# Encoder block with a 32-expert MoE on one Trainium2 core: the branch of an expert's further slots moved ahead of the preceding expert's four down products

## Chip, cores and metric

One core of one Trainium2 chip. The metric is the device time of one execution in microseconds; the kernel before took 2197.92 us, the median of 3 runs (2194.08 to 2198.09).

## The reference, cut to what matters

A streaming-encoder block in float32: 2048 tokens of 1024 numbers. A mixer (mLSTM heads and differential attention) comes first and is not touched by the change. Then a mixture of experts: a token picks one of 4 groups and 2 of its 8 experts, and each of the 32 experts is a SwiGLU with 512 hidden numbers.

```python
g_sel = jnp.argmax(g_logits, axis=-1)
top_vals, top_idx = lax.top_k(e_in, TOP_K)                # 2 of the group's 8
weights = g_w[:, None] * jax.nn.softmax(top_vals, axis=-1)
...
def expert_block(args):
    xb, e = args
    hid = jax.nn.silu(xb @ w_gate[e]) * (xb @ w_up[e])    # 1024 -> 512
    return hid @ w_down[e]                                # 512 -> 1024
...
y = jnp.sum(y_buf[dest].reshape(T, TOP_K, D) * weights[..., None].astype(h.dtype), axis=1)
```

How many tokens an expert gets is known only on the chip. 4096 slots over 32 experts are 128 on average.

## The kernel before

The mixer and the routing fill the first 1388 us. The rest is one unrolled loop over 32 *places* (L1327 on), and an expert stands at each place; a 33rd pass finishes the last one. The order of experts is worked out on the chip, so that those with over 128 slots alternate with others as far as they go.

**The 128 slots that each expert has.** Large products run in split form: a float32 operand is cut into a high part H (ACT, `split_h`, L66) and the rest L (DVE, `split_l`, L70), and H x H, H x L and L x H are added up in PSUM, 3 matmuls for one. `ffn1` (L1231) makes gate and up in 8 steps `d` of 6 matmuls each; `hidden` (L1211 to L1213) makes the hidden numbers `th`, with tanh on ACT and two operations on DVE. The down product of an expert comes one place later: `turn_h` (L1236) turns its th during steps 0 and 1 of the next expert's ffn1, and `down(0)` to `down(3)` (`ffn2`, L1246, 6 matmuls each) stand behind that ffn1. `emit` writes the result one place later still (d = 2: ACT L1251, then a scatter by POOL, L1255, that adds into `out`). During steps 3 and 5 `turn` (L1204) transposes the tokens of the next place, which POOL gathered into `xg0` (L1193); after step 5 POOL gathers those of the place after it.

**Weights.** Raw weights `R` come by SP's DMA queue (L843, `done`), 1 MB a tile, 6 tiles an expert: 4 of gate and up, 2 of down. `ready` splits a half tile 6 halves ahead of its use, into a ring of 4 tiles (8 halves). Each step of ffn1 and each down calls `ready` once, so ACT and DVE get one split a step, in the order of the program.

**Further slots.** An expert with n > 128 enters the branch `more` (L1371). Its further slots go in quarters of Q = 32 rows (M = 64 for the last two), unsplit, against the raw R: `few_turn_x` transposes the tokens (8 small transposes, L1265; ACT copies them to `xH`, L1267), `few_ffn1` is 64 matmuls (L1276) into a `px` tile in PSUM and the `hidden` of it, `few_turn_h` one transpose (L1282) and a copy by ACT to `hH` (L1283), `few_ffn2` 32 matmuls (L1291) into another of the 2 px tiles, `few_emit` four copies by ACT to `yE` (L1307) and a scaling by POOL (L1308), `few_return` the scatter. Inside, `many` (L1376) is n > 160 and `most` (L1384) n > 192. The engines run their own instruction streams: ACT, DVE, POOL and SP take the same branches for themselves. `mark_branch_hint_location` puts a hint (L1458 in the profile) some way ahead of a branch; the branch's If side is the one that falls through, so an expert of up to 128 slots (a *light* place) *takes* the branch to its Else side. In this run 20 places are light, 6 have one quarter, 4 have two and 2 have four.

**Order around the change.** In program order on each engine: ffn1, down(0), down(1), then the branch. Inside it: small transposes, down(2), few_ffn1 of the first quarter, the inner branch; with two quarters or more: small transposes of the second quarter, `few_down` of the first (turn, hH, 32 matmuls), few_ffn1 of the second, yE, down(3), few_down of the second. With one quarter: down(3), then few_down. In a light place: down(2), down(3). The loads of gate and up (`done(e, 0)` to `done(e, 3)`) stand at the end of either side.

Of the kernel before, what the change touches and what calls it, by code (L numbers as in the profile page):

```python
# [19 lines left out]
P = 128  # L20
# [40 lines left out]
def block_kernel(tc, a, out):  # L61
# [44 lines left out]
    with tc.tile_pool(name="const", bufs=1) as cp, tc.tile_pool(name="dram", bufs=1, space=DRAM) as dp:  # L106
# [1060 lines left out]
        with tc.tile_pool(name="mo", bufs=2, reuse_waits="tile") as sp, \  # L1167
# [41 lines left out]
            def hidden(pgu, n, tag=None):  # L1209
                th = sp.tile([P, n], F32, name=f"th{n}", tag=tag or f"th{n}", bufs=1 if tag else 2)  # L1210
                A.activation(th, pgu[:, :n], AF.Tanh, scale=0.5)  # L1211
                V.scalar_tensor_tensor(th, th, 1.0, pgu[:, :n], op0=OP.add, op1=OP.mult)
                V.tensor_tensor(th, pgu[:, n:2 * n], th, OP.mult)  # L1213
                return th
# [55 lines left out]
            def few_ffn1(xH, e, m, c, tag=None):  # L1270
# [7 lines left out]
                return hidden(px, P, tag)  # L1278
# [16 lines left out]
            def few_up(e, m, xH, tag=None):  # L1295
                return [few_ffn1(xH, e, m, c, tag) for c in range(m // Q)]

            def few_down(e, m, th):
                hH = sp.tile([P, 2, P], F32, name="hH", bufs=1)
                for c, t in enumerate(th):  # L1300
                    few_turn_h(t, hH, c)
                return few_ffn2(hH, e, m)
# [24 lines left out]
            for e in range(NE + 1):  # L1327
                u = first_half(e)
                fetch_slots(e + AHEAD)
                if e < NE:  # L1330
# [4 lines left out]
                    for d in range(DC):  # L1335
# [14 lines left out]
                        if d == 4:  # L1350
                            tc.mark_branch_hint_location(f"more{e}", n > P, engines)
# [16 lines left out]
                down(0)  # L1368
                down(1)
                if e < NE:  # L1370
                    with tc.If(n > P, label=f"more{e}", preferred_fallthrough_block=True) as more:  # L1371
                        tc.mark_branch_hint_location(f"more{e}b", n > P + Q, engines)
                        xH = few_turn_x(Q, 0)
                        down(2)
                        ta = few_up(e, Q, xH, "thA")
                        with tc.If(n > P + Q, label=f"more{e}b", preferred_fallthrough_block=True) as many:  # L1376
                            tc.mark_branch_hint_location(f"more{e}c", n > P + M, engines)
                            xH = few_turn_x(Q, Q)
                            pa = few_down(e, Q, ta)
                            tb = few_up(e, Q, xH)  # L1380
                            few_emit(e, Q, 0, pa)
                            down(3)
                            pb = few_down(e, Q, tb)
                            with tc.If(n > P + M, label=f"more{e}c", preferred_fallthrough_block=True) as most:  # L1384
                                xH = few_turn_x(M, M)
                                few_emit(e, Q, Q, pb)
                                few_emit(e, M, M, few_down(e, M, few_up(e, M, xH)))
                                few_return(e, P)
                            with most.Else():
                                few_emit(e, Q, Q, pb)  # L1390
                                few_return(e, M)
                        with many.Else():
                            down(3)
                            few_emit(e, Q, 0, few_down(e, Q, ta))
# [3 lines left out]
                    with more.Else():  # L1398
                        down(2)
                        down(3)  # L1400
                        for j in range(4):
                            done(e, j)
                else:
                    down(2)
                    down(3)
# [56 lines left out]
```

## Time and profile before

| | before |
|---|---|
| median of 3 runs | 2197.92 us (2194.08 to 2198.09) |
| the profiled execution | 2200.45 us, span 2198.6 us |
| mean granted TensorE clock | 0.981 |
| PE busy | 2050.7 us, 93% |
| PEld (weight loads) | 1737.1 us, 79% |
| DVE | 1604.1 us, 73% |
| ACT | 1229.0 us, 56% |
| POOL | 524.6 us, 24% |
| expert loop | from 1388 us to the end |

The rows further down are read from that one profiled execution. Busy shares are means over stages with different limits, so the loop's stretches are read by themselves: a row of the stretches gives the engines' busy time between two times, a row of a group the idle time that its engine spent ahead of it and whose work ended it, and a row of the timeline one instruction, or a few alike, with its start.

### The profile page before, as it was taken

Reading aid. Unit: us, or ns where it says so; the run is one execution under the profiler, and the core shown is the slowest. Engines: PE = TensorE matmul, PEld = TensorE weight load, DVE = VectorE, ACT = ScalarE, POOL = GpSimd, SP = SyncE. Lnnn points to the kernel's source line nnn. Section 1 sums busy time; section 2 is a strip of 40 time slices with the busy share of each in tenths; the row PEclk is TensorE's granted clock in tenths of the full one; section 3 lists DMA queues with packets and bytes.
Section 4 is the critical chain, followed back from the end, with each engine's and each line's share of the span. In section 5 each row is a group of like instructions: output and inputs, shape, how many; then the busy total and the mean of one; then the engine's idle time right before and its main releaser. Section 6 shows DMA issues by size and latency. Waiting matters only on the chain. (4 is left out here: it accounts for less than half of the span.)

```text
span 2198.6 us, 40400 instructions
## 1 busy us (share of the span) xinstructions
PE 2050.7 (93%) x13815; PEld 1737.1 (79%) x13816; DVE 1604.1 (73%) x4373; ACT 1229.0 (56%) x2820; POOL 524.6 (24%) x685
## 2 busy tenths in 40 slices
PE   7999998999999999999999998799998999999986
PEld 6888888898999899999987886677676666666764
DVE  7667655887787688778877777888776656776863
ACT  5434334665566566656653333677675566666663
POOL 4000003322322322232101111232232232323222
PEclk9999999999999999999999999899999999999998
DMA  7555449645553664465228643699997877997972
GB/s 228 179 167 187 140 127 234 186 124 135 167 140 111 176 185 122 129 179 160 82 88 293 230 146 111 227 340 327 330 317 252 286 238 265 321 340 259 349 267 36
DMA packets 241519, 449.69 MB, mean 205 GB/s; under 512 B 36369, under 2 KB 120401, under 8 KB 231249
## 3 DMA queue, kind: packets, MB, share of 16 engines
q1 hardware_dynamic: 192160, 316.56, 42.9%
q0 software_dynamic: 48800, 128.46, 21.9%
q8 instruction: 157, 2.57, 0.5%
q14 instruction: 130, 1.06, 0.1%
q10 hardware_dynamic: 272, 1.05, 0.1%
HBM read 378.51 MB, written 84.25 MB: 210 GB/s over the span
## 5 line engine op out<-in xcount | busy, mean ns | idle before, releaser
L70 DVE TENSOR_TENSOR L<-R,H 128x1024 fp32r<-128x1024 f32 x408 | 484.8, 1223 | 120.1 <-ACT H L66 96.4
L66 ACT ACTIVATE H<-R 128x1024 fp32r<-128x1024 f32 x408 | 414.9, 1057 | 38.2 <-DVE cnti L1158 9.2
L1231 PE MATMUL pgu<-H,xT 128*128 128x512 f32 x1024 | 361.8, 411 | 17.8 <-issue 6.9
L1231 PEld LDWEIGHTS pgu<-H,xT 128*128 128x128 f32 x1024 | 196.9, 192 | 62.2 <-issue 14.8
L585 ACT ACTIVATE prob<-sc,nm 128x512 f32<-128x512 f32 (+3 forms) x320 | 195.8, 623 | 50.6 <-DVE nm L582 45.4
L574 DVE TENSOR_REDUCE mx<-sc 128x1 f32<-128x512 f32 (+3 forms) x320 | 187.3, 604 | 29.8 <-PE sc L570 14.2
L1231 PE MATMUL pgu<-L,xT 128*128 128x512 f32 x512 | 203.7, 398 | 0.0
L570 PE MATMUL sc<-kt,qt 128*128 128x512 f32 (+3 forms) x640 | 190.2, 387 | 8.1 <-DMA kt<-k_d 6.2
L1246 PE MATMUL py<-H,hT 128*128 128x512 f32 x512 | 172.8, 400 | 8.8 <-issue 6.1
L94 PE MATMUL w<-H,hs 128*128 128x256 f32 x512 | 156.2, 305 | 7.1 <-DVE num L690 5.9
L629 PE MATMUL w<-va,aT 128*128 128x128 f32 x1088 | 155.6, 277 | 6.0 <-ACT raw L510 4.4
L500 PE MATMUL w<-hs,H 128*128 128x256 f32 x512 | 157.9, 308 | 2.3 <-ACT tho L545 1.4
L474 POOL DMA_DIRECT2D qt<-q_d x128 | 77.8, 615 | 298.0 <-DMA q_d<-qkT 276.3
L629 PEld LDWEIGHTS w<-va,aT 128*128 128x128 f32 x1088 | 139.3, 191 | 11.3 <-ACT raw L510 7.2
L95 PE MATMUL w<-L,hs 128*128 128x256 f32 x512 | 145.3, 284 | 0.0
L96 PE MATMUL w<-H,hs 128*128 128x256 f32 x512 | 145.1, 283 | 0.0
L501 PE MATMUL w<-hs,H 128*128 128x256 f32 x512 | 144.8, 283 | 0.0
L502 PE MATMUL w<-hs,L 128*128 128x256 f32 x512 | 144.7, 283 | 0.0
L1246 PEld LDWEIGHTS py<-H,hT 128*128 128x128 f32 x512 | 97.4, 190 | 35.5 <-issue 14.2
L1193 POOL DMA_INDIRECT xg<-h_d,ix x64 | 90.3, 1410 | 128.9 <-PE py L1246 46.0
L1308 POOL TENSOR_SCALAR yE<-yE,ix 32x1024 f32<-32x1024 f32 (+1 forms) x20 | 57.0, 2849 | 253.9 <-ACT yE L1307 253.9
L570 PEld LDWEIGHTS sc<-kt,qt 128*128 128x128 f32 x640 | 100.5, 192 | 16.2 <-ACT prob L585 7.4
(374 smaller groups left out, 5241.7 us busy)
## 6 DMA issues: line engine op xcount, KB each, us to landing
R<-w_gate SPq DMA_DIRECT2D x128, 512.0 KB, 10.9
R<-w_up SPq DMA_DIRECT2D x128, 512.0 KB, 11.8
R<-w_down SPq DMA_DIRECT2D x63, 1024.0 KB, 10.3
hs<-hT_d POOLq DMA_DIRECT2D x62, 1024.0 KB, 5.4
hT_d<-hs SPq DMA_DIRECT2D x16, 1024.0 KB, 4.0
qt<-q_d POOLq DMA_DIRECT2D x128, 128.0 KB, 6.2
xt<-x SPq DMA_DIRECT2D x30, 512.0 KB, 4.4
q_d<-qkT SPq DMA_DIRECT2D x32, 256.0 KB, 3.7
```

The costliest lines, as they stand in the source:

```text
L66: return A.activation(dst, src, AF.Copy, scale=scale)
L70: return V.tensor_tensor(dst, src, h.bitcast(F32), OP.subtract)
L94: T.matmul(ps, xh, wh, start=start, stop=False)
L95: T.matmul(ps, xh, wl, start=False, stop=False)
L96: T.matmul(ps, xl, wh, start=False, stop=stop)
L500: T.matmul(ps, l0, m0, start=d == 0, stop=False)
L570: T.matmul(ps[:, :n], QT[g // 2][:, o, m, g % 2 * P:(g % 2 + 1) * P], KT[r * 4 + c][:, m, :n], start=o == 0, stop=o == 1 and c < sb)
L574: V.reduce_max(B["mx"][:, m, c:c + 1], ps[:, :n], axis=AX.X)
L585: mark["ACT"] = A.activation(B["p", m][:, c2 * 512:c2 * 512 + n], B["sc", m, c2][:, :n], AF.Exp, bias=nm, scale=0.125, accum_out=B["rs"][: ...
L629: T.matmul(po, B["aT", c][:, kb * P:(kb + 1) * P], VA[r * 4 + c][:, kb, :], start=c == 0 and kb == 0, stop=c == nch - 1 and kb == nb[c] - 1)
L1231: T.matmul(pgu[c], xT[:, l, d, :], r[:, :, n], start=d == 0 and m == 0, stop=d == DC - 1 and m == 2)
L1246: T.matmul(py[n], hT[:, l, f, :], r[:, c], start=f == 0 and m == 0, stop=f == 3 and m == 2)
```

## The change

The branch on the further slots now stands straight behind ffn1, and its hint behind step 3 and not 4. All four downs stand on each side of it: in a light place one after another; with further slots one by one between the steps of the further slots. `few_down` is taken apart: the turn and the copy (`few_turn`) and `few_ffn2` are now called one by one. The th tile of a quarter has three buffers and no tag of its own, and no px tile is held over into the innermost branch; with four quarters the second quarter's `few_emit` now stands ahead of that branch.

```diff
--- before.py
+++ after.py
@@ -1206,8 +1206,8 @@
                     split_h(xT[:, 0, h, :], pt)
                     split_l(xT[:, 1, h, :], pt, xT[:, 0, h, :])
 
-            def hidden(pgu, n, tag=None):
-                th = sp.tile([P, n], F32, name=f"th{n}", tag=tag or f"th{n}", bufs=1 if tag else 2)
+            def hidden(pgu, n):
+                th = sp.tile([P, n], F32, name=f"th{n}", tag=f"th{n}", bufs=3 if n == P else 2)
                 A.activation(th, pgu[:, :n], AF.Tanh, scale=0.5)
                 V.scalar_tensor_tensor(th, th, 1.0, pgu[:, :n], op0=OP.add, op1=OP.mult)
                 V.tensor_tensor(th, pgu[:, n:2 * n], th, OP.mult)
@@ -1267,7 +1267,7 @@
                     A.activation(xH[:, hf * 4:hf * 4 + 4, :m], pt[:, :, :m], AF.Copy)
                 return xH
 
-            def few_ffn1(xH, e, m, c, tag=None):
+            def few_ffn1(xH, e, m, c):
                 px = pp.tile([P, 512], F32, name="px", bufs=2)
                 for d in range(DC):
                     w = R4[(6 * e + d // 2) % RAWS][:, d % 2 * 1024:(d % 2 + 1) * 1024].rearrange("p (m n) -> p m n", m=2)
@@ -1275,7 +1275,7 @@
                         h = c * 2 + q
                         T.matmul(px[q * m:(q + 1) * m, :2 * P], xH[:, d, :m], w[:, :, h * P:(h + 1) * P],
                                  start=d == 0, stop=d == DC - 1, skip_group_check=True)
-                return hidden(px, P, tag)
+                return hidden(px, P)
 
             def few_turn_h(th, hH, c):
                 pt = pp.tile([P, 4, P], F32, name="pt", bufs=2)
@@ -1292,14 +1292,14 @@
                                  raw[:, q * w:(q + 1) * w], start=f == 0, stop=f == 3, skip_group_check=True)
                 return px
 
-            def few_up(e, m, xH, tag=None):
-                return [few_ffn1(xH, e, m, c, tag) for c in range(m // Q)]
-
-            def few_down(e, m, th):
+            def few_up(e, m, xH):
+                return [few_ffn1(xH, e, m, c) for c in range(m // Q)]
+
+            def few_turn(th):
                 hH = sp.tile([P, 2, P], F32, name="hH", bufs=1)
                 for c, t in enumerate(th):
                     few_turn_h(t, hH, c)
-                return few_ffn2(hH, e, m)
+                return hH
 
             def few_emit(e, m, r0, px):
                 w = D * m // P
@@ -1347,7 +1347,7 @@
                                 gather(IX[e + 2][:, 0], xg0)
                         if d in (3, 5) and e:
                             done(e - 1, 4 + d // 4)
-                        if d == 4:
+                        if d == 3:
                             tc.mark_branch_hint_location(f"more{e}", n > P, engines)
                     thn = [hidden(p, 256) for p in pgu]
                 else:
@@ -1365,44 +1365,47 @@
                         ffn2(py, hT, f, parts(v // 2, v % 2))
                         ready(v + LOOK)
 
-                down(0)
-                down(1)
+
                 if e < NE:
                     with tc.If(n > P, label=f"more{e}", preferred_fallthrough_block=True) as more:
                         tc.mark_branch_hint_location(f"more{e}b", n > P + Q, engines)
                         xH = few_turn_x(Q, 0)
-                        down(2)
-                        ta = few_up(e, Q, xH, "thA")
+                        down(0)
+                        ta = few_up(e, Q, xH)
                         with tc.If(n > P + Q, label=f"more{e}b", preferred_fallthrough_block=True) as many:
                             tc.mark_branch_hint_location(f"more{e}c", n > P + M, engines)
                             xH = few_turn_x(Q, Q)
-                            pa = few_down(e, Q, ta)
+                            down(1)
+                            hH = few_turn(ta)
                             tb = few_up(e, Q, xH)
-                            few_emit(e, Q, 0, pa)
+                            few_emit(e, Q, 0, few_ffn2(hH, e, Q))
+                            down(2)
+                            hH = few_turn(tb)
                             down(3)
-                            pb = few_down(e, Q, tb)
+                            few_emit(e, Q, Q, few_ffn2(hH, e, Q))
                             with tc.If(n > P + M, label=f"more{e}c", preferred_fallthrough_block=True) as most:
                                 xH = few_turn_x(M, M)
-                                few_emit(e, Q, Q, pb)
-                                few_emit(e, M, M, few_down(e, M, few_up(e, M, xH)))
+                                few_emit(e, M, M, few_ffn2(few_turn(few_up(e, M, xH)), e, M))
                                 few_return(e, P)
                             with most.Else():
-                                few_emit(e, Q, Q, pb)
                                 few_return(e, M)
                         with many.Else():
+                            down(1)
+                            hH = few_turn(ta)
+                            down(2)
+                            few_emit(e, Q, 0, few_ffn2(hH, e, Q))
                             down(3)
-                            few_emit(e, Q, 0, few_down(e, Q, ta))
                             few_return(e, Q)
                         for j in range(4):
                             done(e, j)
                     with more.Else():
-                        down(2)
-                        down(3)
+                        for f in range(4):
+                            down(f)
                         for j in range(4):
                             done(e, j)
                 else:
-                    down(2)
-                    down(3)
+                    for f in range(4):
+                        down(f)
                 if e:
                     waiting = (py, IX[e - 1][:, 0])
                 if e < NE:
```

**PE, two or more quarters, the turn of the first quarter's th** (names: `py` the down products' result, `H_`, `L_` and `R_` weight tiles with their buffer numbers). Before, from the small transposes of the second quarter on:

```order
L1265 MATMUL pt<-ident,xg_18096 128x32 x8
L1282 MATMUL pt<-ident,th_19281 128x128
L1291 MATMUL px<-R_15367,hH 32x256 x8
L1291 MATMUL px<-R_15368,hH 32x256 x8
L1276 MATMUL px<-R_112,xH 32x256 x8
```

and now:

```order
L1265 MATMUL pt<-ident,xg_18096 128x32 x8
L1246 MATMUL py_18694<-H_113,hT 128x512
L1246 MATMUL py_18694<-L_115,hT 128x512
L1246 MATMUL py_18694<-H_113,hT 128x512
L1246 MATMUL py_18695<-H_113,hT 128x512
L1246 MATMUL py_18695<-L_115,hT 128x512
L1246 MATMUL py_18695<-H_113,hT 128x512
L1282 MATMUL pt<-ident,th_18763 128x128
L1276 MATMUL px<-R_15369,xH 32x256 x8
```

A down (down(1)) now stands between the small transposes and the turn, and the 64 matmuls of the second quarter stand ahead of the 32 (L1291) that read hH.

**ACT, the same block, from the copies of the second quarter's tokens to the inner branch.** Before:

```order
L1267 ACTIVATE xH<-pt 128x4x32 x2
L1283 ACTIVATE hH<-pt 128x128
L1211 ACTIVATE th_18868<-px 128x128
L1307 ACTIVATE yE<-px 32x256 x4
L66 ACTIVATE H_113<-R_15365 128x1024
L1283 ACTIVATE hH<-pt 128x128
L1384 COMPARE_AND_BRANCH
```

and now:

```order
L1267 ACTIVATE xH<-pt 128x4x32 x2
L66 ACTIVATE H_3617<-R_15364 128x1024
L1283 ACTIVATE hH<-pt 128x128
L1211 ACTIVATE th_18838<-px 128x128
L1307 ACTIVATE yE<-px 32x256 x4
L66 ACTIVATE H_113<-R_15365 128x1024
L1283 ACTIVATE hH<-pt 128x128
L66 ACTIVATE H_113<-R_15365 128x1024
L1307 ACTIVATE yE<-px 32x256 x4
L1386 COMPARE_AND_BRANCH
```

A split (L66) now comes ahead of each hH (the first belongs to down(1)'s `ready`, the next two to those of down(2) and down(3)), and the four copies to yE of the second quarter stand ahead of the innermost branch, with the copies of the M slots' tokens behind them.

**PE, ffn1, the hint of the outer branch** (- before, + now), from step 3's turn on:

```order
 L1204 MATMUL pt<-ident,xg_18095 128x128 x4
+L1351 REGISTER_ALU
+L1461 BRANCH_PREFETCH_HINT
 L1231 MATMUL pgu<-H_3615,xT 128x512
 L1231 MATMUL pgu<-L_3616,xT 128x512
 L1231 MATMUL pgu<-H_3615,xT 128x512 x2
 L1231 MATMUL pgu<-L_3616,xT 128x512
-L1231 MATMUL pgu<-H_3615,xT 128x512
-L1351 REGISTER_ALU
-L1458 BRANCH_PREFETCH_HINT
-L1231 MATMUL pgu<-H_3615,xT 128x512
+L1231 MATMUL pgu<-H_3615,xT 128x512 x2
```

The hint stands one step (6 matmuls) sooner in the instruction stream. Behind ffn1 the branch now follows at once, where two downs (12 matmuls) stood ahead of it: 24 large matmuls and 4 transposes lie between hint and branch, where it was 30 and 4.

## Rows read from the trace of the kernel before

**Rows 1.** The page: span, then busy time, share and instructions of PE

```profile
span 2198.6 us, 40400 instructions
...
PE 2050.7 (93%) x13815; PEld 1737.1 (79%) x13816; DVE 1604.1 (73%) x4373; ACT 1229.0 (56%) x2820; POOL 524.6 (24%) x685
```

**Rows 2.** Stretches: light place 6, then places 5, 13, 18 and 12

```profile
core 0: us, PE busy (x) PEld busy (x) DVE busy (x) ACT busy (x) POOL busy (x), PEclk, DMA share, GB/s
1510.40:1528.30 17.90, 17.90 (x88) 14.76 (x85) 14.71 (x18) 17.39 (x25) 10.47 (x6) 1.00 1.00 336
1483.40:1510.40 27.00, 24.87 (x190) 17.86 (x189) 20.69 (x25) 15.40 (x23) 3.14 (x3) 1.00 0.95 313
1665.10:1712.50 47.40, 43.04 (x386) 28.41 (x384) 21.66 (x30) 20.84 (x41) 9.15 (x4) 1.00 0.59 209
1819.90:1854.40 34.50, 31.01 (x296) 21.72 (x294) 18.44 (x24) 18.64 (x34) 6.30 (x3) 1.00 0.60 213
1643.30:1665.10 21.80, 19.53 (x85) 15.71 (x84) 17.99 (x22) 15.15 (x20) 6.84 (x5) 0.92 1.05 347
```

**Rows 3.** Groups of PE in the expert loop: busy, mean ns, idle before, releaser

```profile
L1246 PE MATMUL py<-H,hT 128*128 128x512 f32 x512 | 172.8, 400 | 8.8 <-issue 6.1 <-ACT H L66 2.1 <-ACT hT L66 0.6
...
L1291 PE MATMUL px<-R,hH 128*32 128x256 f32 (+1 forms) x608 | 43.7, 405 | 16.5 <-ACT hH L1283 16.5
...
L1204 PE MATMUL pt<-ident,xg 128*128 128x128 f32 x248 | 37.4, 273 | 13.1 <-DMA xg<-h_d,ix 9.6 <-DVE hT L70 3.5
...
L1282 PE MATMUL pt<-ident,th 128*128 128x128 f32 x22 | 6.7, 303 | 4.7 <-DVE th L1213 4.7
```

**Rows 4.** Timeline of place 13 (four quarters), PE and ACT: start, duration, instruction

```profile
1687.26 0.30 PE L1282 MATMUL pt<-ident,th 128*128 128x128 f32 x1 [0.53 <-DVE th L1213]
...
1687.92 1.93 PE L1291 MATMUL px<-R,hH 128*32 128x256 f32 x32 [0.37 <-ACT hH L1283]
...
1693.24 0.50 PE L1246 MATMUL py<-H,hT 128*128 128x512 f32 x1
...
1693.55 1.53 ACT L1307 ACTIVATE yE<-px 32x256 f32<-32x256 f32 x4
...
1696.38 1.93 PE L1291 MATMUL px<-R,hH 128*32 128x256 f32 x32 [1.37 <-ACT hH L1283]
...
1699.18 3.67 PE L1276 MATMUL px<-R,xH 128*64 128x256 f32 x32 [0.23 <-ACT xH L1267]
...
1703.96 3.67 PE L1276 MATMUL px<-R,xH 128*64 128x256 f32 x32 [1.11 <-DVE th L1213]
```

**Rows 5.** Timeline of place 8 (one quarter), PE, behind the inner branch

```profile
1573.84 0.80 PE L1246 MATMUL py<-H,hT 128*128 128x512 f32 x1 [2.33 <-issue]
...
1577.35 1.93 PE L1291 MATMUL px<-R,hH 128*32 128x256 f32 x32 [0.37 <-ACT hH L1283]
```

**Rows 6.** Timelines: POOL behind place 3, then L1204 of places 5 and 12

```profile
1477.93 2.35 POOL L1255 DMA_INDIRECT out<-y,ix  x1 [4.10 <-DMA out<-yE,ix]
1480.58 1.05 POOL L1193 DMA_INDIRECT xg<-h_d,ix  x1 [0.30 <-issue]
...
1491.29 0.63 PE L1204 MATMUL pt<-ident,xg 128*128 128x128 f32 x4 [1.73 <-DMA xg<-h_d,ix]
...
1651.70 0.63 PE L1204 MATMUL pt<-ident,xg 128*128 128x128 f32 x4 [2.27 <-DMA xg<-h_d,ix]
```

**Rows 7.** Outer branch, hint (ns min/median/max, starts), first matmul behind it, place 17

```profile
L1371 PEldq COMPARE_BRANCH  x43: 77/197/6134, 1396.9 to 2171.2; - x43
...
L1458 PEldq BRANCH_PREFETCH_HINT  x1: 40/40/40, 1804.3 to 1804.3; - x1
...
L1371 PEldq COMPARE_BRANCH  x1: 3237/3237/3237, 1541.1 to 1541.1; - x1
...
L1371 PEldq COMPARE_BRANCH  x1: 6134/6134/6134, 1809.2 to 1809.2; - x1
...
L1371 PEldq COMPARE_BRANCH  x1: 3710/3710/3710, 1865.5 to 1865.5; - x1
...
L1371 PEldq COMPARE_BRANCH  x1: 4569/4569/4569, 1932.6 to 1932.6; - x1
...
1815.53 0.47 PE L1246 MATMUL py<-H,hT 128*128 128x512 f32 x1 [2.06 <-ACT H L66]
```

## The prediction, made before the changed kernel had run

> **What bounds it now.** The page comes first. TensorE (PE) is busy 93% of the span [rows 1], so a gain must come from PE's idle time or from slow PE work. Next come stretches of single places. A light place between calm neighbours is 17.90 us long with PE busy for all of it; the 16 DMA engines are full as well [rows 2]. A one-quarter place is 27.00 us, PE busy 24.87; a four-quarter place 47.40, PE 43.04; a two-quarter place 34.50, PE 31.01. So the heavy places have idle PE time, 2 to 4 us each, and there the DMA engines are not full in the two- and four-quarter ones (0.60) but nearly so in the one-quarter ones (0.95). The expert loop's PE groups then say what ends the waits [rows 3]: L1291 (second product of the further slots) lost 16.5 us to ACT's hH, L1282 4.7 us to DVE's th, L1204 (turning the next place's tokens) 13.1, the down products L1246 8.8, of which 6.1 is "issue". The order of experts gives 6 places with one quarter (3, 5, 8, 10, 20, 23), 4 with two (18, 25, 28, 30), 2 with four (13, 15) and 20 light ones.
>
> One down is 6 of the 72 large matmuls of a light place: (17.90 us less 16 transposes at about 0.1) / 72 is 0.226 us, times 6 is 1.36 us, an estimate from [rows 2] used throughout.
>
> **(a) Places with two or four quarters (6).** The four-quarter place shows three waits that the other five have in the same size [rows 4]: 0.53 us at the turn of the first quarter's th, 0.37 at its hH, 1.37 at the second quarter's hH. After the change down(1) stands ahead of the first turn and few_up ahead of the first L1291, so 1.36 us covers 0.53 and 3.64 us covers 0.37: gain 6 x 0.90 = 5.4. The third wait comes from ACT's order: yE (1.53), a split, then hH. From the start of down(3) at 1693.24, right behind the matmuls that yE waits for, to the start of the second L1291 at 1696.38 it is 3.14. After the change PE has down(2), a turn of 0.27 and down(3) to do in that stretch, 1.36 + 0.27 + 1.36 = 3.0, and ACT the same three steps. Some 0.15 stays, 0.25 with a gap between instructions; gain 6 x 1.12 = 6.7, at worst 0 (if a late split holds hH back), at best 8.2. Sum **-12.1**, between -5.4 and -13.6.
>
> **(b) The two four-quarter places.** The held px buffer made the second M product wait 1.11 for th [rows 4]; it is now free: -2.2. Against it, yE of the second quarter (1.53) now runs on ACT ahead of the M slots' xH, which PE awaited 0.23: +1.45 each, +2.9. Sum **+0.7**, between -2.2 and +2.9.
>
> **(c) One-quarter places (6).** down(2) now stands between the turn and L1291, where place 8 waited 0.37 for hH [rows 5]. L1291's 16.5 [rows 3] are 6 x 1.74 of (a), 5 such waits of 0.37, and 4.2 that are left for one longer wait, at place 20. I take 0.37 at each of the six. Sum **-2.2**, between 0 and -3.6 (all of a down, 1.36, off the long one, and at the other five another 0.07 of the turn with the 0.37). The 2.33 us of "issue" at the first down after the inner branch [rows 5] stay: hint and inner branch are as far apart as before (8 small turns, one down, 64 matmuls).
>
> **(d) The next places' tokens.** Behind a one-quarter place POOL's queue is a chain: yE, its scatter, the gather, the scatter of y, which waited 4.10 us for out<-yE, and behind it the gather into xg0 [rows 6]. PE waits for that gather at L1204: 1.73 at place 5, 2.27 at place 12, and as much at 7 and 10 between them. yE of a one-quarter place now leaves before down(3), 1.36 us sooner against the end of the place. The whole chain can move by at most that; I take 1.0 at four places, as landing times vary by more than the shift. Place 12, with the longest wait, ran at a mean granted clock of 0.92, with 19.53 us of PE work [rows 2]: a shorter wait also saves some of that, 1.0 (0 to 1.6 = 19.53 less 17.90). Sum **-5.0**, between 0 and -7.
>
> **(e) The outer branch.** The hint, which I take to begin the fetch of the branch's target, now stands 24 large matmuls and a turn ahead of the branch, not 30: 1.36 us less. PE's sequencer spent from 0.08 to 6.13 us in an outer branch [rows 7], the long ones in light places, where it is taken. At place 17 the hint came at 1804.3 and the branch at 1809.2; it ended 6.13 later, at 1815.3, and PE's array, which had been fed ahead, stood idle for 2.06 until 1815.53. So about 4.07 us of a taken branch lie behind matmuls already issued, and a branch must exceed 4.07 to show. Above 2.7 now, and so above 4.07 with 1.36 more, are four: 6.13 (17), 4.57 (22), 3.71 (19), 3.24 (7) [rows 7]. At 17 and 7 PE has just waited for tokens at L1204, behind which the hint now stands; the sequencer then hurries to the branch, and I take twice the shift, 2.7. Price: 17 +2.7, 7 3.24 + 2.7 - 4.07 = +1.9, 22 +1.36, 19 3.71 + 1.36 - 4.07 = +1.0. Sum **+7.0**, from 0 (if the target arrives as soon after the branch as before) to +10 (slow matmuls behind each stall).
>
> [...]
>
> **At nothing.** The downs' own work, the loads' releases (at most 1.4 us earlier in a one-quarter place), the third th buffer, and the joins behind the two-quarter blocks, which wait as before. The gathered tokens of the further slots are needed two downs (2.7 us) sooner: their gather stands at the head of a place in POOL's program, a gather was followed by its reader 10.7 us later (1480.58 to 1491.29 [rows 6]), and the small transposes now come some 12.5 us in (48 matmuls of 0.226 and 16 transposes), so nothing.
>
> **Sum:** -12.1 + 0.7 - 2.2 - 5.0 + 7.0 = -11.6. The profiled execution took 2200.45 us, with a span of 2198.6 [rows 1]; 2188.85 on that base. The median shown, 2197.92, is 2.53 lower: **2186.3**. Own range 2179 to 2193.
>
> **Rivals.**
> *R1, the loads are the bound where the one-quarter places stand.* For: DMA is 1.00 to 1.05 busy in the light places and 0.95 in a one-quarter one [rows 2]; there PE time saved only meets the next weights earlier, and becomes a wait at the split. Against: in a light place with DMA full PE still never waits. Then (c) and (d) bring nothing: -12.1 + 0.7 + 7 = -4.4: 2193.5. Much the same time comes out if hH stays late in (a): 6.7 worse than the forecast, 2193.7.
>
> *R2, slower: the fetch at the taken branch.* Place: PE, first down of a light place. If the sequencer's lead elsewhere is less than the 4.07 us that one place shows, each of 19 light places with downs shows up to its 1.36: 19 x 1.36 = 25.8 against gains of 12.1 - 0.7 + 2.2 + 5.0 = 18.6: +7.2, **2205**. It decides from 18.6 / 19, about 1.0 us shown per light place. For: 6.13 and 4.57 us branches already show. Against: the median of all outer branch records is 0.197 us [rows 7], far from 4.
>
> *R3, the fetch is no later.* If the target arrives a fixed time after the branch is known, or the shorter distance is covered everywhere: (e) is 0 and the sum -18.6, **2179**; with all bounds at their best 2173.
>
> **Chances.** Forecast 0.55, R1 0.17, R2 0.15, R3 0.13. What a measurement here can tell from no change is 0.2%, 4.4 us: "same" is 2193.5 to 2202.3. Of the forecast's 0.55, 0.03 lies above 2193.5. Faster 0.52 + 0.13 = 0.65, same 0.17 + 0.03 = 0.20, slower 0.15. The range, 2173 to 2203, holds the forecast, R1, R3 with its best bounds, and the lower edge of R2.
>
> **What would show it.** (a) L1291's idle time before from 16.5 to about 6, L1282's 4.7 under 2; (b) L1276's wait no longer named after DVE th, but ACT xH, about 1.7 at places 13 and 15; (d) L1204's 13.1 under 10; (e) L1246's idle in light places up by 4 to 7 us with "issue" or ACT H as its end, and outer branches of over 4 us at four or five places. I am wrong if L1246's idle grows by over 18 us (R2), if DVE or ACT waits for R at the splits take up the gain (R1), or if heavy places don't shorten: about 2 us each in (a), 0.4 in (c).

## The result and the profile after

The changed kernel takes **2169.74 us** (median of 4 runs, 2168.61 to 2173.22), the kernel before 2196.99 (4 runs). The ratio is 0.9876, 95% interval 0.9859 to 0.9892: 27 us faster, more than twice the gain forecast, and 3 us below the lower end of the forecast's range.

The profiled execution went from a span of 2198.6 to 2166.9 us, 31.7 less. Of these, 2.8 lie ahead of the expert loop, where the two programs are alike (its first matmul stands at 1387.83 before and at 1385.02 now; over the profiles of this study that start varies between 1385.0 and 1390.3). The loop went from 810.8 to 781.9 us, 28.9 less. The page of the kernel after, span and first row; it answers to [rows 1]:

```profile
span 2166.9 us, 40488 instructions
...
PE 2048.8 (95%) x13815; PEld 1735.3 (80%) x13816; DVE 1603.8 (74%) x4373; ACT 1230.9 (57%) x2820; POOL 517.1 (24%) x685
```

PE's busy time is the same within 2 us, so the gain is PE's idle time. [rows 3] leaves out two groups of the loop before (busy, mean ns, idle before, releasers):

```profile
L1231 PE MATMUL pgu<-H,xT 128*128 128x512 f32 x1024 | 361.8, 411 | 17.8 <-issue 6.9 <-DVE L L70 4.1 <-ACT yE L1307 2.4
...
L1276 PE MATMUL px<-R,xH 128*32 128x256 f32 (+1 forms) x1280 | 80.4, 380 | 2.7 <-DVE th L1213 2.2 <-ACT xH L1267 0.4
```

The groups after, against these and [rows 3]:

```profile
L1231 PE MATMUL pgu<-H,xT 128*128 128x512 f32 x1021 | 358.1, 409 | 14.2 <-issue 5.9 <-DVE L L70 5.2 <-DVE th L1213 2.2
L1246 PE MATMUL py<-H,hT 128*128 128x512 f32 x512 | 177.2, 409 | 11.8 <-issue 10.2 <-ACT th L1211 0.8 <-ACT hT L66 0.6
L1246 PE MATMUL py<-L,hT 128*128 128x512 f32 x256 | 101.9, 398 | 1.6 <-issue 1.6
L1276 PE MATMUL px<-R,xH 128*32 128x256 f32 (+1 forms) x1280 | 80.1, 381 | 2.9 <-ACT xH L1267 2.9
L1291 PE MATMUL px<-R,hH 128*32 128x256 f32 (+1 forms) x608 | 42.6, 394 | 2.2 <-issue 2.2
L1204 PE MATMUL pt<-ident,xg 128*128 128x128 f32 x248 | 37.3, 273 | 3.3 <-DMA xg<-h_d,ix 3.2
...
L1282 PE MATMUL pt<-ident,th 128*128 128x128 f32 x22 | 6.4, 292 | 1.7 <-DVE th L1213 1.7
```

Read the number behind the second bar, and set it beside the kernel before:

| PE idle ahead of | before | after | change |
|---|---|---|---|
| L1291, second product of the further slots | 16.5 | 2.2 | -14.3 |
| L1282, turn of their th | 4.7 | 1.7 | -3.0 |
| L1276, their first product | 2.7 | 2.9 | +0.2 |
| L1204, turn of the next place's tokens | 13.1 | 3.3 | -9.8 |
| L1246, downs (both forms) | 8.8 | 13.4 | +4.6 |
| L1231, ffn1 | 17.8 | 14.2 | -3.6 |
| L1236, turn of th | 0.9 | 0.0 | -0.9 |
| sum | 64.5 | 37.7 | -26.8 |

The table is read from 1388 us on in both. Counted from each loop's own start, 26.5 of its 28.9 us are idle time that is gone, and PE's busy time is 2.0 less. The stretches of single places, against [rows 2] (places 6, 5, 13, 18 and 12; the columns are the same):

```profile
1508.92:1527.40 18.48, 18.07 (x85) 14.57 (x84) 16.64 (x20) 17.41 (x23) 9.95 (x6) 1.00 1.01 339
1481.15:1508.92 27.77, 24.84 (x190) 17.89 (x189) 19.34 (x24) 15.48 (x26) 3.74 (x2) 1.00 0.90 313
1651.18:1696.14 44.96, 42.68 (x385) 27.92 (x383) 21.89 (x30) 22.03 (x42) 9.15 (x4) 1.00 0.69 250
1798.81:1832.46 33.65, 30.84 (x295) 21.53 (x294) 20.44 (x26) 19.56 (x37) 7.42 (x4) 1.00 0.75 269
1633.03:1651.18 18.15, 18.03 (x85) 14.53 (x84) 17.24 (x21) 14.48 (x21) 4.48 (x3) 1.00 1.05 350
```

Place 13 is 2.4 us shorter, place 18 0.9 (more was idle at its join, below), place 12 3.7, its granted clock 1.00 where it was 0.92. But place 5 is 0.8 us *longer*, though its 1.73 us wait for tokens is gone: the stall at its inner branch grew from nothing to 2.92. The branch on PE's sequencer, and the first matmul behind it:

```profile
L1375 PEldq COMPARE_BRANCH  x1: 4326/4326/4326, 1498.1 to 1498.1; - x1
...
1502.47 0.50 PE L1246 MATMUL py<-H,hT 128*128 128x512 f32 x1 [2.92 <-issue]
```

The DMA share of 1.05 and the place of 18.15 stand side by side at place 12, so full DMA engines did not hold the gain back (R1).

The waits of [rows 4], in the timeline of place 13 after (PE):

```profile
1671.48 0.27 PE L1282 MATMUL pt<-ident,th 128*128 128x128 f32 x1
...
1675.16 1.91 PE L1291 MATMUL px<-R,hH 128*32 128x256 f32 x32
...
1680.09 1.93 PE L1291 MATMUL px<-R,hH 128*32 128x256 f32 x32
1681.95 0.71 PE L1265 MATMUL pt<-ident,xg 64*128 64x64 f32 x8
1684.09 7.13 PE L1276 MATMUL px<-R,xH 128*64 128x256 f32 x64 [1.43 <-ACT xH L1267]
```

No bracket stands behind the first three: 0.53, 0.37 and 1.37 us are gone altogether. The M slots' xH is now awaited 1.43 us, where it was 0.23 and then 1.11 for th.

POOL behind place 3 and PE's turn of tokens at place 5, against [rows 6]:

```profile
1474.55 1.60 POOL L1255 DMA_INDIRECT out<-y,ix  x1 [4.71 <-ACT xT L66]
1476.45 1.70 POOL L1193 DMA_INDIRECT xg<-h_d,ix  x1 [0.30 <-PE py L1246]
...
1487.16 0.63 PE L1204 MATMUL pt<-ident,xg 128*128 128x128 f32 x4
```

Place 4 began at 1463.36 (at 1465.55 before), so the gather into xg0 now starts 13.1 us into it and not 15.0; its reader at place 5 doesn't wait.

The outer branch, against [rows 7]: all of its records on PE's sequencer, that of place 17, and the first down behind it:

```profile
L1370 PEldq COMPARE_BRANCH  x43: 73/314/4035, 1395.4 to 2137.1; - x43
...
L1370 PEldq COMPARE_BRANCH  x1: 3792/3792/3792, 1789.3 to 1789.3; - x1
...
1793.24 0.47 PE L1246 MATMUL py<-H,hT 128*128 128x512 f32 x1 [0.15 <-ACT th L1211]
```

The longest is 4.04 us; place 17 has 3.79, not 6.13, and PE waited 0.15 us behind it, not 2.06.

### The profile page after: what moved, and what is told of

It is laid out like the page before. It is cut to its first block, busy times and chain, and to the rows that moved or that the text cites. A ratio compares the mean times of both kernels' runs of the same rounds, so it can differ in the third digit from the quotient of the medians.

```text
span 2166.9 us, 40488 instructions
## 1 busy us (share of the span) xinstructions
PE 2048.8 (95%) x13815; PEld 1735.3 (80%) x13816; DVE 1603.8 (74%) x4373; ACT 1230.9 (57%) x2820; POOL 517.1 (24%) x685
## 3 DMA queue, kind: packets, MB, share of 16 engines
q14 instruction: 133, 1.09, 0.1%
q10 hardware_dynamic: 272, 1.05, 0.1%
## 5 line engine op out<-in xcount | busy, mean ns | idle before, releaser
L66 ACT ACTIVATE H<-R 128x1024 fp32r<-128x1024 f32 x408 | 415.8, 1056 | 27.8 <-DVE cnti L1158 9.2
L1231 PE MATMUL pgu<-H,xT 128*128 128x512 f32 x1024 | 360.1, 410 | 14.4 <-issue 5.9
L1231 PEld LDWEIGHTS pgu<-H,xT 128*128 128x128 f32 x1024 | 196.1, 192 | 57.5 <-issue 15.7
L574 DVE TENSOR_REDUCE mx<-sc 128x1 f32<-128x512 f32 (+3 forms) x320 | 186.9, 602 | 32.4 <-PE sc L573 16.5
L1231 PE MATMUL pgu<-L,xT 128*128 128x512 f32 x512 | 203.0, 397 | 0.0
L1246 PE MATMUL py<-H,hT 128*128 128x512 f32 x512 | 177.2, 409 | 11.8 <-issue 10.2
L629 PEld LDWEIGHTS w<-va,aT 128*128 128x128 f32 x1088 | 139.3, 191 | 11.6 <-ACT raw L510 7.3
L1246 PEld LDWEIGHTS py<-H,hT 128*128 128x128 f32 x512 | 98.2, 192 | 45.1 <-issue 23.1
```

Of the source, the lines that this page charges most:

```text
L66: return A.activation(dst, src, AF.Copy, scale=scale)
L574: V.reduce_max(B["mx"][:, m, c:c + 1], ps[:, :n], axis=AX.X)
L629: T.matmul(po, B["aT", c][:, kb * P:(kb + 1) * P], VA[r * 4 + c][:, kb, :], start=c == 0 and kb == 0, stop=c == nch - 1 and kb == nb[c] - 1)
L1231: T.matmul(pgu[c], xT[:, l, d, :], r[:, :, n], start=d == 0 and m == 0, stop=d == DC - 1 and m == 2)
L1246: T.matmul(py[n], hT[:, l, f, :], r[:, c], start=f == 0 and m == 0, stop=f == 3 and m == 2)
```

## The experiments

Nine kernels besides the changed one were run. Ratios are against the kernel before, with 95% intervals; the changed kernel's own is 0.9859 to 0.9892.

| run | median us | interval of the ratio |
|---|---|---|
| e1, quarters in the old order | 2184.42 | 0.9917 to 0.9953 |
| e2, yE last | 2181.11 | 0.9908 to 0.9937 |
| e3, hint behind step 4 | 2176.79 | 0.9876 to 0.9913 |
| e4, the kernel before with yE first | 2191.37 | 0.9965 to 0.9990 |
| e5, hint behind step 6 | 2216.60 | 1.0052 to 1.0104 |
| e6, hint behind step 1 | 2164.89 | 0.9801 to 0.9884 |
| v1, down(1) ahead of the inner branch | 2170.08 | 0.9849 to 0.9897 |
| v2, v1 and down(3) last | 2158.79 | 0.9791 to 0.9844 |
| v3, v2 and hint behind step 1 | 2157.86 | 0.9782 to 0.9860 |

**e1: the order of the quarters.**

```diff
                             xH = few_turn_x(Q, Q)
-                            down(1)
-                            hH = few_turn(ta)
+                            pa = few_ffn2(few_turn(ta), e, Q)
                             tb = few_up(e, Q, xH)
-                            few_emit(e, Q, 0, few_ffn2(hH, e, Q))
+                            few_emit(e, Q, 0, pa)
+                            down(1)
                             down(2)
-                            hH = few_turn(tb)
                             down(3)
+                            hH = few_turn(tb)
```

Expected:

> The changed kernel, but with two or more quarters the further slots' steps stand in the order of before (turn and second product of the first quarter ahead of the first product of the second; its yE ahead of the downs; downs 1, 2 and 3 in a row ahead of the turn of the second). Theory: the waits 0.53, 0.37 and 1.37 us were on the path, so they come back at 6 places: L1282's idle time up by about 3, L1291's by about 10, time up by 11 to 14 us, to 2181 to 2184. Rival (the gain came from where the branch stands, or from fetches): time within 3 us of the changed kernel, 2167 to 2173.

Measured 2184.42, 14.7 us above the changed kernel, the intervals apart. The two groups of PE in its loop:

```profile
L1291 PE MATMUL px<-R,hH 128*32 128x256 f32 (+1 forms) x608 | 43.2, 397 | 7.3 <-ACT hH L1283 5.4 <-issue 2.0
...
L1282 PE MATMUL pt<-ident,th 128*128 128x128 f32 x22 | 6.8, 307 | 4.9 <-DVE th L1213 4.9
```

L1282's wait came back as expected (+3.2). L1291's came back by 5.1, not 10: three downs now stand between the two products, and the third wait is 0.53 and not 1.37. So the profile shows 8.6 us of waits (6 x (0.53 + 0.37 + 0.53)), and the loop of the profiled execution is 10.0 us longer. The order of the quarters is on the path, and it is worth its waits, some 10 us in the loop. The rest of the 14.7 no row of the loop accounts for: in these two profiled executions 5.3 us of the difference lie ahead of the loop (it starts at 1390.3 and 1385.0), where the programs are alike.

**e2 and e4: where yE stands in a one-quarter place.** e2 is the changed kernel with

```diff
                             down(2)
-                            few_emit(e, Q, 0, few_ffn2(hH, e, Q))
                             down(3)
+                            few_emit(e, Q, 0, few_ffn2(hH, e, Q))
```

> The changed kernel, but in a one-quarter place down(3) stands ahead of the second product and yE, so that yE leaves 1.36 us later against the end of the place. Theory: the tokens' waits at L1204 went because POOL's chain behind yE starts sooner; L1204's idle time goes from 3.3 to 10 or more, time up by 6 to 10 us, 2176 to 2180. Rival (the waits went for another reason, such as place-to-place shifts of the transfers): L1204 stays under 5, time within 2 us of the changed kernel.

e4 is the kernel before with

```diff
-                            down(3)
                             few_emit(e, Q, 0, few_down(e, Q, ta))
+                            down(3)
                             few_return(e, Q)
```

> The kernel before with one edit: in a one-quarter place yE and its product stand ahead of down(3). Theory: L1204's idle time falls from 13.1 to under 6; the uncovered turn and hH cost at most 1 us more in each of 6 places (L1282 and L1291 up by 3 to 6); slow matmuls behind the long waits go too. Time down by 3 to 8 us, 2189 to 2194. Rival (yE's place is worth nothing): L1204 above 10 and time up by 2 to 6 us from the uncovered waits.

e2 took 2181.11, 11.4 us more than the changed kernel, above the 6 to 10 expected. Its group for L1204 in the loop:

```profile
L1204 PE MATMUL pt<-ident,xg 128*128 128x128 f32 x251 | 38.3, 275 | 13.2 <-DMA xg<-h_d,ix 13.1
```

One down in another place brings back 9.9 us of waits for tokens: 3.3 to 13.2, as many as before the change. They stand where the chain behind a one-quarter place ends, two places later: 5.6 us at 5, 7, 10 and 12, and 4.8 at 22 and 25. The loop of the profiled execution is 6.2 us longer (788.0 us) and not 9.9, as 4.4 us of the changed kernel's stalls at L1291, L1246 and L1231 are not in it. So yE's place is worth somewhere between these 6.2 and the 11.4 of the medians. In e4 the same edit the other way round, and nothing else:

```profile
L1204 PE MATMUL pt<-ident,xg 128*128 128x128 f32 x248 | 37.5, 274 | 7.4 <-DVE hT L70 3.1 <-DVE L L70 2.3 <-DMA xg<-h_d,ix 1.9
...
L1282 PE MATMUL pt<-ident,th 128*128 128x128 f32 x22 | 6.6, 298 | 14.8 <-DVE th L1213 9.6 <-issue 5.1
...
L1291 PE MATMUL px<-R,hH 128*32 128x256 f32 (+1 forms) x608 | 44.3, 410 | 12.9 <-ACT hH L1283 12.9
```

At the four places 5, 7, 10 and 12 the waits fell from 7.9 us to 1.8 (0, 0.33, 1.09 and 0.41); over the loop from 13.1 to 7.4, a little short of the "under 6" expected. The turn and hH, with no down to cover them, show 6.5 us more idle time (21.2 to 27.7 in L1282 and L1291); most of that is the inner branch's stall, now ahead of L1282 and no longer of L1246, whose idle time fell by 5.4 (8.8 to 3.4). Net 5.8 us, in the range expected. So yE's place alone frees most of the tokens' waits, in either kernel; what the change adds to it is that the turn and hH stay covered.

**e3, e5, e6: the hint of the outer branch**, moved by the one number in `if d == 3`.

> The changed kernel with the hint of the outer branch behind step 4 again, so with 18 large matmuls between it and the branch. Theory (a hint's distance is paid in the branch, but up to about 4 us of it lie behind matmuls already issued): the taken outer branches, 40.7 us together in the changed kernel, go up by some 20 us or more, the shown part up by 3 to 10 us, time 2173 to 2180. Rival (the fetch does not begin at the hint): branches and time as in the changed kernel, within 2 us.

> The changed kernel with the hint of the outer branch behind step 6, so that 6 large matmuls lie between hint and branch. Theory (the target arrives some 6.5 us after the hint, mean of the changed kernel, and about 4 us of a taken branch lie behind matmuls already issued): the sequencer meets the branch 1 to 2 us after the hint, a taken branch takes about 5 us, 100 us over 20 places, and 0.5 to 2 us of it show at each: time up by 10 to 35 us, 2180 to 2205. Rival (the fetch begins at the branch, or the hint does nothing): branches as in the changed kernel, 2.0 us on average, time within 3 us of it.

> The changed kernel with the hint of the outer branch behind step 1, two steps sooner. Theory (in the changed kernel the target arrives in time: no taken outer branch is long enough to show): branches get shorter, near their floor of 0.4 us at most places, but PE's idle time in the downs of light places, 2.3 us in all, is all that can go: time within 3 us of the changed kernel, 2167 to 2172. Rival (the 1.36 us that the change took from the lead cost the 7 us that I forecast): 2161 to 2165.

Over the 20 light places, PE's sequencer (means worked out from the records of hints and branches; the last column is the sum of the two ahead of it, from the hint to the end of the branch):

| hint behind step | lead, hint to branch, us | taken branch, us | target there after the hint, us |
|---|---|---|---|
| 4, with two downs more (before) | 6.25 | 1.62 | 7.9 |
| 3 (changed kernel) | 4.51 | 2.03 | 6.5 |
| 4 (e3) | 4.15 | 2.35 | 6.5 |
| 6 (e5) | 1.27 | 5.60 | 6.9 |

e3 didn't tell what it was meant to. My expectation counted 18 matmuls as lead; the lead in the sequencer's own time fell by 0.36 us only, and what holds the sequencer isn't shown. The time, 2176.79, was within the range expected, but the branches rose by 6.3 us in all and not 20, and its interval overlaps that of the changed kernel: inconclusive. One row of it counts all the same. At place 24, where the changed kernel had a branch of 3.91 us and 0.29 shown, the target came 10.4 us after the hint:

```profile
L1370 PEldq COMPARE_BRANCH  x1: 6077/6077/6077, 1966.1 to 1966.1; - x1
...
1972.38 0.47 PE L1246 MATMUL py<-H,hT 128*128 128x512 f32 x1 [2.45 <-ACT H L66]
```

So the late target of place 17 before is not gone for good; it can come back at another place.

e5 did tell. With 1.27 us of lead the branches grew to 112 us together. One of them, at place 4, the first down behind it, and the stretch of that place:

```profile
L1370 PEldq COMPARE_BRANCH  x1: 6141/6141/6141, 1480.8 to 1480.8; - x1
...
1487.11 0.47 PE L1246 MATMUL py<-H,hT 128*128 128x512 f32 x1 [2.51 <-ACT H L66]
```

```profile
1472.11:1494.28 22.17, 19.66 (x86) 15.72 (x84) 18.73 (x22) 17.56 (x23) 10.75 (x6) 0.92 1.03 342
```

The bracket names ACT, but the branch ended at 1480.8 + 6.1 = 1486.9, and PE went on at 1487.1. The place is 22.17 us long, 4.4 more than the 17.8 that place has in the changed kernel: 2.51 idle, and 1.9 of slow matmuls (19.66 us busy, where it was 17.79; granted clock 0.92). Not every such wait slows the matmuls: place 24 had 2.62 idle and kept its clock and its busy time, 18.06 as in the changed kernel:

```profile
1986.58:2007.26 20.68, 18.06 (x86) 14.57 (x84) 18.71 (x22) 17.55 (x23) 10.11 (x6) 1.00 1.03 342
```

Over the loop of the profiled execution PE was idle 30.5 us more than in the changed kernel, and busy 15.1 more (745.6 for 730.5). That is why the 2216.60 lie above the 2180 to 2205 expected: I had priced the wait alone. In these three runs the time to the target counts from the hint and not from the branch: with mean leads of 1.27 (e5), 4.15 (e3) and 4.51 us (changed kernel) the target is there 6.9, 6.5 and 6.5 us behind the hint, and a taken branch takes 5.60, 2.35 and 2.03.

e6, with the hint two steps sooner (mean lead 9.08 us), has 16 of 20 taken branches at 0.5 us or less, and 2164.89 us. The other four still took 1.6 to 3.5 us, with 8.3 to 9.0 us of lead: their targets came 10.2 to 12.6 us after the hint, so 6.5 is no fixed time. The 2164.89 lie 4.8 us below the changed kernel, but the intervals overlap, and the two profiled spans are 2166.4 and 2166.9. They lie below the theory's 2167 and within the upper end of the rival's 2161 to 2165, so e6 doesn't settle the last few microseconds; the 2.6 us of idle time in L1246 that went (13.4 to 10.8) are what its profile shows:

```profile
L1246 PE MATMUL py<-H,hT 128*128 128x512 f32 x512 | 176.2, 407 | 10.8 <-issue 10.2 <-ACT hT L66 0.6
```

**v1 and v2: can more be had?** v1, against the changed kernel (`...` marks what is left out):

```diff
                         ta = few_up(e, Q, xH)
+                        down(1)
...
                             xH = few_turn_x(Q, Q)
-                            down(1)
+                            down(2)
                             hH = few_turn(ta)
                             tb = few_up(e, Q, xH)
-                            few_emit(e, Q, 0, few_ffn2(hH, e, Q))
-                            down(2)
+                            pa = few_ffn2(hH, e, Q)
                             hH = few_turn(tb)
+                            few_emit(e, Q, 0, pa)
                             down(3)
...
                         with many.Else():
-                            down(1)
                             hH = few_turn(ta)
```

> The changed kernel with down(1) ahead of the inner branch (6 large matmuls more between its hint and it), and with two or more quarters down(2) in its old place and the second quarter's turn and hH ahead of the first quarter's yE. Theory: the inner branch's shown stalls, 10.2 us at places 5, 20 and 23, shrink by 1.36 us each or more, the slow matmuls behind them too, no new wait over 0.4 us: time down by 4 to 8 us, 2162 to 2166. Rival (stalls follow the layout of the code, not the distance): they move to other places with the same sum, time within 3 us of the changed kernel.

2170.08: as the changed kernel; the rival's case. The stall at the inner branch went from L1246 to L1282:

```profile
L1282 PE MATMUL pt<-ident,th 128*128 128x128 f32 x22 | 6.8, 308 | 13.0 <-issue 9.9 <-DVE th L1213 1.7 <-DVE L L70 1.5
```

A down more does cover more: a branch of 5.03 us shows 2.34 at place 5, where one of 4.33 showed 2.92, so 2.7 us lie behind issued matmuls and not 1.4. But five of the six one-quarter places now have a branch of over 4 us, where three had; the sum shown is 11.3 us, and was 10.2. L1291's stall at place 10 (2.2) went, but the waits for tokens rose from 3.3 to 7.0. Why the branch takes longer there isn't shown, and no run shows whether it follows the layout of the code.

v2 has v1's edits, but down(3) leaves its place ahead of the second quarter's product and stands behind the innermost branch:

```diff
                             with tc.If(n > P + M, label=f"more{e}c", preferred_fallthrough_block=True) as most:
                                 xH = few_turn_x(M, M)
+                                down(3)
...
                             with most.Else():
+                                down(3)
                                 few_return(e, M)
```

> As the run before, but with two or more quarters down(3) stands last, behind the innermost branch (with four quarters between the M slots' transposes and their product). Theory: with two quarters the stalls at the join to the next place (2.81, 3.06, 5.17 and 0.98 us in the changed kernel) shrink by 1.4 us or more each, and the slow matmuls behind them, the M slots' wait of 1.43 for xH goes at 2 places; against it hH of the second quarter is awaited 0.37 us at 6 places: time down by 4 to 10 us against the run before, 2154 to 2162. Rival (the join's stall is a wait for other engines' work, not a fetch): it stays, and the time is 0 to 2 us above the run before.

2158.79, 11 us below the changed kernel and clear of it: the fastest order with its hint where the change put it. Its groups:

```profile
L1231 PE MATMUL pgu<-H,xT 128*128 128x512 f32 x1024 | 355.4, 405 | 6.1 <-ACT H L66 4.0 <-DVE th L1213 2.2
...
L1276 PE MATMUL px<-R,xH 128*32 128x256 f32 (+1 forms) x1280 | 80.1, 381 | 0.0
...
L1282 PE MATMUL pt<-ident,th 128*128 128x128 f32 x22 | 6.7, 307 | 10.5 <-issue 6.1 <-DVE L L70 2.7 <-DVE th L1213 1.7
```

L1231's idle time fell from 14.2 to 6.1: the stalls at the joins behind the two-quarter places, 12.0 us in the changed kernel (2.81, 3.06, 5.17 and 0.98), are 4.0 (1.23, 1.41, 1.35 and none). The branch that ends these blocks took the sequencer 1.70, 2.03, 4.12 and 0.19 us in the changed kernel, and 0.19, 0.19, 3.05 and 0.19 in v2, where 6 large matmuls issued straight ahead of it keep PE at work meanwhile. Only part of the gain is idle time: in the loop of the profiled execution (768.3 us for 781.9) PE is idle 8.7 us less, and busy 5.7 less (724.8 for 730.5), at a granted clock of 0.99 where it was 0.97. The M slots' wait is gone (L1276 at 0.0), and hH of the second quarter is awaited 0.43 at each of 6 places, near the 0.37 expected.

v3 is v2 with the hint behind step 1:

> The faster version (down(1) ahead of the inner branch, down(3) last with two or more quarters) with the hint of the outer branch behind step 1. Theory: as it is, 2156 to 2161; what is left idle in it (8 us for the gathered tokens, 10 at the inner branch) does not hang on this hint. Rival: 5 to 8 us less.

2157.86: as v2.

## Why the prediction was wrong, step by step

The direction was right and the size wrong: 11.6 us forecast, 27 measured. Two terms of the sum failed, (d) in its size and (e) in its sign; the gain in (c) is in part luck.

**(a)** held, and came to its better end. The three waits of 2.27 us a place went in full, -13.6 idle (forecast -12.1). e1 shows them on the path: with them partly back, the loop is 10.0 us longer.

**(b)** held: 2 x (-1.11 + 1.20 at xH + 0.09 at the M slots' turn) = +0.4, forecast +0.7. The second yE cost 1.20 to 1.29 each of its 1.53 us; the 1.45 in the sum wasn't worked out.

**(c)** was right for five waits of 0.37. At place 20 the 4.2 at hH are gone, but a stall of 4.20 stands ahead of the first down behind the inner branch. The old wait had a cause of its own: ACT began the split ahead of that hH late, after 4.31 us in which it waited for nothing that the profile shows.

```profile
1899.03 1.06 ACT L66 ACTIVATE H<-R 128x1024 fp32r<-128x1024 f32 x1 [4.31 <-issue]
```

One down (1.36 us) put in its way can't have covered it, and e4, with the old order up to yE's place, doesn't have it either (0.43). Why ACT was late is open, and that this wait went is luck.

**(d) failed in its size.** The step was "The whole chain can move by at most that; I take 1.0 at four places, as landing times vary by more than the shift". The 1.36 us was no bound, and a share of it was the wrong price. Behind place 3 the gather started 1.9 us sooner against the start of place 4: 1.5 for yE, and the rest in shorter issues and waits of the POOL instructions between. Behind the four one-quarter places it landed 1.9 to 2.6 us sooner. The waits at 5, 7, 10 and 12, none above 2.3, went in full: 7.9 us of idle time for the 4.0 forecast, and place 12's matmuls came 1.5 us quicker for the 1.0 forecast. e2 shows the cause, with 6.2 us in the loop and 11.4 by the medians, where (d) said 5.0. L1204 as a whole lost 9.8 us; its waits at 20 and 27 (3.1), behind two-quarter places, went too, for a reason not shown, and 15 and 17 gained 1.1. In these runs a wait behind a chain didn't shrink by a share of the shift: the whole shift counted, until the wait was gone.

**(e) failed in its sign.** The step was to take the four longest branches of the kernel before (17, 22, 19 and 7) and lengthen them by what the lead lost. In e5 a microsecond of lead did cost about one of branch (3.24 less lead, 3.57 more branch). That the same targets would be late again was wrong. In the trace of before the target of place 17 came 11.1 us after the hint, at 19 and 22 10.5 and 10.7; in the changed kernel these three came 6.5, 6.9 and 6.3 after it, and no target took over 8.4. Beside this stand the records of the DMA queue q8, which the profile lists as one of instructions: an outer branch of a light place that took over 0.6 us ended 2.3 to 2.6 us after the start of the last q8 packet ahead of its end, in both traces, and that packet started 8.1 to 8.6 us after the hint in the three late cases, but at most 6.0 after it in the changed kernel. Why such a packet starts late is open, so that none was late in the changed kernel is luck as far as these runs show; e3, one step of the hint away, has one at place 24 (10.4). The 4.07 us that (e) took to lie behind issued matmuls were 3.6 in the changed kernel: branches of 4.04 and 3.91 showed 0.41 and 0.29. So the outer branches' stalls of 2.06 and 0.52 us went, where (e) added 7.0; against them stand 0.4 and 0.3 us at places 6 and 24, and 1.65 us of "issue" among the downs of place 22, where the next packet of q8 started 2.4 us before PE went on.

**At nothing** hid two things that roughly balance. The inner branch's stalls ahead of the downs rose from 5.6 us (2.33, 0.86 and 2.39 at places 8, 10 and 23) to 10.2 (2.92, 4.20 and 3.03 at 5, 20 and 23), though hint and branch have as many instructions between them as before, and the lead is 7.9 us where it was 8.3; (c) had said that they stay. And of L1231's 3.6 us, 2.3 are the wait for ACT's split at place 8's start, where ACT had waited 1.80 for a load of R, and which isn't there now; another 1.5 are an "issue" stall at place 23.

**The sum.** (a) to (c) gave 17.1 us of idle time for 13.6 forecast, (d) 9.8 for 4.0 and clock; (e) was to take 7.0 and came out about even (2.6 gone, 2.4 new). Of the 17.1, 4.2 are the lucky wait at place 20, and the stalls of the inner branch took as much again. By whole times e1 (14.7) and e2 (11.4) add up to 26.1 of the 27.3 us, but by the loops of their profiled executions to 10.0 and 6.2 of 28.9. So these two causes are shown; that they make up the whole gain isn't.

**The rivals.** R3, no fetch later, was the nearest at 2179; its best bounds still fell short, with (d) capped at 7. As listed they add up to -26.4, so to 2171.5 and not the 2173 written (and a late hH in (a) comes to 2193.0, not 2193.7). An outer branch has no one price in these runs: not taken it took 73 to 89 ns in the traces before and after, taken from 0.37 us there to the 7.15 of e5. R2's state exists: e5 has it, with 5.60 us a taken branch and a time 18 us above the kernel before. But it needed about 1.0 us shown at each light place, and the changed kernel, with leads of 2.7 to 5.8 us, shows 0.97 of the 40.7 us of its taken outer branches as idle time of PE. R1 is out: the one-quarter places and those behind them gained most of (d) with the DMA engines as full as before.

## What to carry to other kernels

Look for work that needn't stand where it does (here a down product) and put it where an engine waits, but choose its place also by what starts behind it: the product whose result heads another queue's chain goes first, the filler last. Price a wait behind a chain by the whole shift, up to the length of the wait, not by a share. Give a branch's hint its lead in the sequencer's own time, read from the trace, with some to spare: 1.27 us of it left a mean taken branch of 5.60 us (e5), 9.08 us left 16 of 20 at 0.5 us or less (e6), and the target's time isn't fixed (up to 11.1 us before, 12.6 in e6). Have large matmuls issued when a branch is met: behind them 3.6 to 4.1 us of it did not show, behind the small ones of the inner branch 1.4. And put long work that is already issued last ahead of a jump: in v2, 6 large matmuls there went with stalls of 4.0 us at the joins, where they were 12.0.

## What the runs showed of the hardware that was not expected

- The end of a taken outer branch came 6.5 us after its hint on average in the changed kernel (5.1 to 8.4) and 6.9 in e5, but up to 11.1 before, 10.4 in e3 and 12.6 in e6. Before and in the changed kernel, those of over 0.6 us ended 2.3 to 2.6 us after the start of the last q8 packet ahead of that end.
- 6 large matmuls fewer between hint and branch (1.36 us by the prediction's estimate) cost 0.36 us of lead in e3.
- Part of a late branch showed no idle time of PE, which had matmuls issued ahead of it: 4.1 us behind the downs (places 17 and 22 before), 3.6 behind ffn1 in the changed kernel (4.04 us shown as 0.41) and in e5 (6.14 as 2.51), 1.4 behind the small matmuls of the inner branch (4.33 shown as 2.92, 5.60 as 4.20, 4.43 as 3.03), 2.7 with one down behind them.
- One idle stretch of PE went with more than itself: in e5 place 4 had 2.51 us idle, ran at a granted clock of 0.92 and needed 4.4 us more. But place 24, with 2.62 idle, kept its full clock; what tells the two apart isn't shown.
